# A chunked linear recurrence in a two-layer decoder trunk: the merge emitted ahead of the next preparation, and preparation and substitution emitted among the chunk loop

## The chip, the cores and the metric

The kernel runs on one core of a Trainium2 chip. The metric is the device time of one execution in microseconds (us). A core has five engines with queues of their own: TensorE (PE in the profile, its weight loads PEld), VectorE (DVE), ScalarE (ACT), GpSimd (POOL) and SyncE (SP). SP computes nothing here; it issues the DMA transfers. Each engine works off its own queue in the order in which the program put it there, and waits where an instruction needs a result or a buffer that is not there yet.

## The reference, cut to what matters

A trunk of two layers over 1024 positions of width 1024. Layer 0 mixes tokens by a gated MLP, layer 1 by a recurrence with a state of 64x64 per head (16 heads). Behind each mixer come a cross-attention and a SwiGLU feed-forward network. The change touches the recurrence of layer 1 alone:

```python
def rwkv7_recurrence(r, w, k, v, a, b):
    """S_t = S_{t-1} diag(w_t) + (S_{t-1} a_t) b_t^T + v_t k_t^T ;  y_t = S_t r_t."""
    def step(S, inp):
        r_t, w_t, k_t, v_t, a_t, b_t = inp
        sa = jnp.einsum('bhij,bhj->bhi', S, a_t)
        S = S * w_t[:, :, None, :] + sa[..., None] * b_t[:, :, None, :] + v_t[..., None] * k_t[:, :, None, :]
        return S, jnp.einsum('bhij,bhj->bhi', S, r_t)
    ...
    _, y = lax.scan(step, S0, xs)

def rwkv7_time_mix(...):
    ...
    y = rwkv7_recurrence(rh, decay, kh, vh, -kk, kk * ah)
    # group norm of y per head, bonus term, gate, output projection
    return (y * g) @ w_o, v_first
```

## The kernel before

The 1024 positions of the recurrence are cut into four batches b of 256 positions, and a batch into four chunks of 64. In a chunk the recurrence becomes matrix products once a triangular system of 64x64 per head and chunk is inverted. Heads are worked in pairs: eight pairs p, and groups pi of two pairs. Five steps, each a Python generator that stops (yields) after a small piece of work, make one batch:

- **Preparation** (`rwkv_prep`, L1280 to L1356), once per group pi: loads five inputs from DRAM (L1292), a running sum and exponentials (L1295, L1298), products (L1307 to L1311), then on PE the bonus sums (L1318), the score blocks (L1330, masked by DVE in L1333), transposes (L1337) and products with the values (L1354). The diagonal blocks of the triangular systems go to DRAM (L1343, L1344).
- **Substitution** (`rwkv_solve`, L1361 to L1385), once per batch: reads the diagonal blocks of all four groups back (L1366) and inverts the 32x32 triangles by 31 dependent steps of two DVE instructions each (L1376, L1377), then writes the result to DRAM (L1381, L1384).
- **Merge** (`rwkv_merge`, L1387 to L1423): reads the inverses back (L1393, L1398) and joins two 32x32 inverses to one of 64x64, by 64 and 64 products on PE (L1410, L1419; the profile counts each float32 product twice) with copies by ACT between them (L1413, L1422). The result lies in two buffers `Z` that all batches share.
- **Chunks** (`rwkv_chunks`, L1425 to L1482): 32 small chains per batch (four chunks by eight pairs), each a product with the state (L1446), an addition on DVE (L1447), a product with Z and further products (L1433), with ACT copying results and the new state (L1453, L1462, L1465). Chunk c of a pair needs the state that chunk c-1 left.
- **Post** (`rwkv_post`, L1484 to L1531): group norm of the outputs on DVE and POOL (L1498 to L1513), transposes on PE (L1520, L1527), the gate (L1528, L1529) and a store to DRAM.

Batch b's chunks need its merge, this its substitution, and this the whole preparation of the batch. The function `rwkv` (L1533) puts the steps in order. `run(g)` takes all pieces of a generator one after another and lets one piece of each waiting queue of tasks in behind each (`tick`); `later(g, q)` puts a generator into such a queue; `drain` empties the queues. What is emitted in this way is an order of priorities and no more: the framework's scheduler takes it together with its own model of times and of free buffers, and lays down each engine's queue from it. So instructions of one step can stand in a queue far ahead of steps that were emitted before it. Buffers that are reused (four PSUM banks `ps` for preparation and post, four `ck` for merge and chunks, 32 tiles `a`, seven `ld` and four `lx` for loaded inputs, one `invA` and one `invZ` that substitution and merge share) decide with it.

Of the kernel before, what the change touches and what calls it, by code (L numbers as in the profile page):

```python
# [21 lines left out]
class Trunk:  # L22
# [1510 lines left out]
    def rwkv(self, W, C, filler, mk_close):  # L1533
        nc = self.nc
        B = [self.rwkv_batch() for _ in range(4)]
        R, states = ({}, {})
        left, top, right = (ExitStack(), ExitStack(), ExitStack())

        def pools(stack, side, *nb):
            for n, bufs in nb:  # L1540
                R[n] = stack.enter_context(self.tc.tile_pool(name='r' + n, bufs=bufs, reuse_waits='tile', side=side))

        def stagger(gens, lag):

            gens = list(gens)
            done = [False] * len(gens)
            n = 0
            while not all(done):
                for i, g in enumerate(gens):
                    if n >= i * lag and (not done[i]):  # L1550
                        try:
                            next(g)
                        except StopIteration:
                            done[i] = True
                n += 1
                yield

        def prep(b):
            return stagger([self.rwkv_prep(R, B[b], pi, b, D_[0], C) for pi in range(4)], 7 if b else 6)

        def chunks(b):
            yield from self.rwkv_chunks(R, B[b], b, states)

        def post(b):
            return stagger([self.rwkv_post(R, B[b], pi, b, D_[0], C) for pi in range(4)], 2 if b == 3 else 1)

        def run(*gens, rate=1):
            for g in gens:
                for _ in g:
                    self.tick(rate)  # L1570

        def gated(half):

            xh, xl = self.chunks()
            for k in range(KD):
                t = R['ld'].tile([P, 512], F32, name='zt', tag='ld')
                nc.sync.dma_start(t, D_[0]['z'][k, :, half * 512:half * 512 + 512])
                self.split(xh[k], xl[k], t)
            return (xh, xl)
        D_ = []  # L1580

        def before_last():
            self.close_main()
            pools(left, 'left', ('inv', 1), ('D', 8))
            self.rwkv_consts(left.enter_context(self.tc.tile_pool(name='rconst', bufs=1, reuse_waits='tile', side='left')), C)
            pools(left, 'left', ('ld', 7))
            pools(top, 'left', ('tt', 4))
            self.open_main(2, 3, 2)
            self.open_psum(4, 4)
            self.later(prep(0))  # L1590
        d, gate_out = self.rwkv_project(W, C, filler, before_last, D_)
        self.drain()
        run(self.rwkv_solve(R, B[0]))
        p1 = prep(1)
        self.later(p1)
        gate_out()
        self.close_main()
        pools(top, 'left', ('bk', 4))
        pools(right, 'right', ('z', 1), ('st', 1), ('lx', 4))
        R['Z'] = [R['z'].tile([P, 2, 8, 64], F32, name=f'z{i}', tag=f'z{i}') for i in range(2)]  # L1600
        R['rs'] = [[R['st'].tile([P, P], F32, name='rs', tag=f'rs{h}{i}') for i in range(4)] for h in range(2)]
        for x in R['rs'][0] + R['rs'][1]:
            nc.gpsimd.memset(x, 0.0)
        for z in R['Z']:
            nc.gpsimd.memset(z[32:64, :, :, 0:32], 0.0)
            nc.gpsimd.memset(z[96:128, :, :, 0:32], 0.0)
        run(self.rwkv_merge(R, B[0]), p1)
        for b in range(1, 4):
            o = 3
            sv = self.rwkv_solve(R, B[b])  # L1610
            if o in (0, 1):
                run(sv, chunks(b - 1))
            elif o in (2, 3):
                run(chunks(b - 1), sv)
            else:
                self.later(sv)
                run(chunks(b - 1), rate=1)
                self.drain(0)
            self.later(post(b - 1), 1)
            if b == 3:  # L1620
                break
            if o in (0, 2, 4):
                run(self.rwkv_merge(R, B[b]))
            run(prep(b + 1), rate=1)
            if o in (1, 3, 5):
                run(self.rwkv_merge(R, B[b]))
            self.drain()
        top.close()
        self.open_main(2, 2, 1, 'left')
        gain, tmp = (self.gain_bc, self.tmp)  # L1630
        self.gain_bc = lambda row: gain(row, self.a32())
        self.tmp = self.a32
        for _ in range(2):
            self.tick()
        close = mk_close()
        x = gated(0)

        def between():
            run(self.rwkv_merge(R, B[3]))
            self.drain()  # L1640
            run(chunks(3))
            self.later(post(3), 1)
        first = self.out_half(x, 0, W['o'], close, 4, between)
        self.drain()
        self.open_psum(8)
        x = gated(1)
        self.later(first, 1)
        second = self.out_half(x, 1, W['o'], close)
        self.drain()
        self.gain_bc, self.tmp = (gain, tmp)  # L1650
        self.close_main()
        right.close()
        left.close()
        self.open_main(3, 4, 4, s7=2)
        self.later(second)
# [71 lines left out]
```

## Time and profile before

| | |
|---|---|
| median of three runs | 3225.27 us (3217.7 to 3227.76) |
| profiled execution, its own time | 3225.86 us |
| its span, first to last instruction | 3224.2 us |
| granted PE clock, mean | 0.966 |
| DVE, ACT, POOL busy | 1825.7, 1485.6, 824.9 us |

The loop over batches that the change rewrites lies between 1852 us and 2121 us of the span; the last merge and the last chunks (L1639 to L1641) follow, beside the output projection. In the profile a row of a list of groups has line, engine, operation, output and inputs, then the count, the busy time and the mean duration of one. A row of a list of instructions in order of time has start and duration, and in brackets how long the engine stood idle before it and what released it. In a table of stretches PEclk is the granted clock as a share of full speed.

### The profile page before, as it was taken

To read this page: it belongs to the slowest core of one execution; us is meant where nothing else is said; L and a number is where in the kernel's file an instruction comes from. 1 tells how busy PE (TensorE), PEld (TensorE's weight loads), DVE (VectorE), ACT (ScalarE), POOL (GpSimd) and SP (SyncE) were. 2 spreads that over 40 slices of the span, in tenths; PEclk is the share of its full clock that TensorE was granted. 3 is DMA by queue.
4 is the path that set the end of the run, shared out by engine and by line. 5 is a ranking of instruction groups with operands and counts; after the bars stand their busy time and mean duration, and the time that the engine had idled before them with its cause. 6 is when DMAs were issued, how large, how long until landed. Compare 5 with 4: busy or idle time off the path is not lost.

```text
span 3224.2 us, 43854 instructions
## 1 busy us (share of the span) xinstructions
PE 3085.9 (96%) x16570; PEld 2523.5 (78%) x16570; DVE 1825.7 (57%) x2562; ACT 1485.6 (46%) x2751; POOL 824.9 (26%) x646
## 2 busy tenths in 40 slices
PE   8999999899999999999989999999999899999998
PEld 6888888778888777878767778787788678888776
DVE  5563544565555476655765665664545755554656
ACT  5442544543333345666653445455545533333443
POOL 0100011355555100111421121223011555554001
PEclk9999999999999999999998888899999999999999
DMA  5622634423333644744857642535544333333633
GB/s 188 207 77 67 201 122 161 144 66 104 105 98 99 243 142 131 222 122 151 260 190 194 192 107 81 153 96 179 175 153 142 100 102 98 98 98 114 237 112 134
DMA packets 432499, 456.54 MB, mean 142 GB/s; under 512 B 77664, under 2 KB 307200, under 8 KB 432288
## 3 DMA queue, kind: packets, MB, share of 16 engines
q1 hardware_dynamic: 425376, 428.57, 42.2%
q0 software_dynamic: 6912, 25.17, 2.4%
q8 instruction: 131, 2.15, 0.3%
q14 instruction: 80, 0.66, 0.1%
HBM read 331.43 MB, written 122.22 MB: 141 GB/s over the span
## 4 chain that ended last, share of the span: by engine, by line
PE 83%; DVE 7%; DMA 4%; ACT 2%; issue 2%; POOL 1%; SPq 1%; DVEq 0%; POOLq 0%; ACTq 0%
PE ps L438 25%; PE ps L148 12%; PE ps L149 12%; PE ps L150 12%; PE ps L639 11%; PE ck L1433 4%; DVE wl L119 2%; PE ps L1330 2%; PE ck L1446 1%; PE ps L1354 1%; DVE a L119 1%; ACT wh L118 1%; PE ps L262 1%; DMA a<-scr 1%; PE ps L1337 1%
## 5 line engine op out<-in xcount | busy, mean ns | idle before, releaser
L438 PE MATMUL ps<-a,wh 128*128 128x512 f32 x2464 | 772.6, 399 | 7.2 <-DVE a L119 5.0
L119 DVE TENSOR_TENSOR wl<-wr,wh 128x1024 fp32r<-128x1024 f32 (+1 forms) x417 | 478.9, 1158 | 485.9 <-ACT wh L118 477.7
L118 ACT CAST wh<-wr 128x1024 fp32r<-128x1024 f32 (+1 forms) x417 | 371.3, 902 | 621.7 <-PE ps L639 172.6
L438 PEld LDWEIGHTS ps<-a,wh 128*128 128x128 f32 x2464 | 465.6, 189 | 125.6 <-DVE a L119 7.3
L438 PE MATMUL ps<-a,wl 128*128 128x512 f32 x1232 | 480.3, 398 | 0.0
L148 PE MATMUL ps<-a,wh 128*128 128x512 f32 (+1 forms) x848 | 329.1, 393 | 11.3 <-ACT a L118 8.0
L149 PE MATMUL ps<-a,wh 128*128 128x512 f32 (+1 forms) x848 | 326.2, 386 | 2.4 <-DVE a L119 2.4
L148 PE MATMUL ps<-wh,a 128*128 128x512 f32 x800 | 316.4, 403 | 12.3 <-DVE a L1528 3.9
L150 PE MATMUL ps<-a,wl 128*128 128x512 f32 (+1 forms) x848 | 325.0, 385 | 0.8 <-DVE wl L119 0.8
L149 PE MATMUL ps<-wl,a 128*128 128x512 f32 x800 | 319.2, 399 | 0.8 <-DVE wl L119 0.8
L150 PE MATMUL ps<-wh,a 128*128 128x512 f32 x800 | 317.2, 400 | 0.0
L208 POOL TENSOR_TENSOR sm<-sm,mhalf 128x4 f32<-128x4 f32 (+3 forms) x60 | 70.0, 1170 | 922.0 <-DVE sm L228 846.4
L438 PEld LDWEIGHTS ps<-a,wl 128*128 128x128 f32 x1232 | 233.2, 189 | 57.3 <-DVE wl L119 0.9
L639 PE MATMUL ps<-wl,wh 128*128 128x512 f32 x588 | 233.0, 396 | 11.6 <-DVE wl L119 11.6
L119 DVE TENSOR_TENSOR wl<-s,wh 128x512 fp32r<-128x512 f32 x176 | 201.1, 1156 | 68.4 <-ACT wh L118 64.7
L639 PE MATMUL ps<-wh,wl 128*128 128x512 f32 x588 | 230.9, 393 | 0.0
L639 PE MATMUL ps<-wh 128*128 128x512 f32 x588 | 195.3, 395 | 15.1 <-ACT wh L118 15.1
L118 ACT CAST wh<-s 128x512 fp32r<-128x512 f32 x176 | 106.3, 620 | 201.8 <-PE ps L438 66.9
L148 PEld LDWEIGHTS ps<-a,wh 128*128 128x128 f32 x848 | 163.0, 193 | 44.0 <-ACT a L118 9.0
L148 PEld LDWEIGHTS ps<-wh,a 128*128 128x128 f32 x800 | 152.3, 191 | 49.5 <-DVE a L1528 4.3
L150 PEld LDWEIGHTS ps<-a,wl 128*128 128x128 f32 x848 | 163.0, 192 | 35.4 <-DVE wl L119 2.3
L149 PEld LDWEIGHTS ps<-a,wh 128*128 128x128 f32 x848 | 163.4, 193 | 32.9 <-DVE a L119 2.7
(280 smaller groups left out, 5338.2 us busy)
## 6 DMA issues: line engine op xcount, KB each, us to landing
scr<-a SPq DMA_DIRECT2D x218, 256.0 KB
wr<-in_ffn_w_in SPq DMA_DIRECT2D x90, 512.0 KB
wr<-scr SPq DMA_DIRECT2D x70, 512.0 KB
scr<-t SPq DMA_DIRECT2D x60, 512.0 KB
wr<-in_rw_w_rkv SPq DMA_DIRECT2D x48, 512.0 KB
a<-in_ffn_w_out SPq DMA_DIRECT2D x40, 512.0 KB
t<-scr SPq DMA_DIRECT2D x36, 512.0 KB
ld<-scr SPq DMA_DIRECT2D x72, 256.0 KB
```

What stands on the lines that cost most here:

```text
L118: self.nc.scalar.copy(hi, src)
L119: (engine or self.nc.vector).tensor_sub(lo, src, hi)
L148: nc.tensor.matmul(out, lhsT=ah, rhs=bh, start=start, stop=False)
L149: nc.tensor.matmul(out, lhsT=ah, rhs=bl, start=False, stop=False)
L150: nc.tensor.matmul(out, lhsT=al, rhs=bh, start=False, stop=stop)
L208: self.nc.gpsimd.tensor_tensor(out=r, in0=v, in1=self.mhalf[:, 0:n], op=ALU.pow)
L262: nc.tensor.transpose(ps[:, t * P:(t + 1) * P], xs[t][:, k * P:(k + 1) * P], self.ident)
L438: self.nc.tensor.matmul(out, lhsT=a, rhs=b, start=start and k == 0 and (i == 0), stop=k == 3 and i == 2, skip_group_check=True)
L639: nc.tensor.matmul(ps, lhsT=a, rhs=b, start=i in (1, 2, 5) and n == 0 and k == 0 and z == 0, stop=n == NS - 1 and k == steps[n][1] - 1 and ...
L1330: nc.tensor.matmul(ps[:, c * P:(c + 1) * P], lhsT=BK[hs, q * 4 + c, :, :], rhs=AR[hs, q * 4 + c, :, :], start=True, stop=True)
L1337: nc.tensor.transpose(ps[:, c * P:(c + 1) * P], BK[:, q * 4 + c, :, :], self.ident)
L1433: mm = lambda o, l, r: nc.tensor.matmul(o, lhsT=l, rhs=r, start=False, stop=True, skip_group_check=True)
```

## The change

The loop over batches is written anew. Before, the order of emission for each b from 1 is: chunks of b-1, substitution of b, preparation of b+1 (with post of b-1 as a task beside it), merge of b. After, it is: post of b-1 becomes a task, merge of b, and then chunks of b with two pieces of "preparation of b+1, then substitution of b+1" behind each piece of chunks. The first batch's chunks and the second's substitution are emitted as before, and so are the third batch's post and what follows.

```diff
-        for b in range(1, 4):
-            o = 3
-            sv = self.rwkv_solve(R, B[b])
...
-            elif o in (2, 3):
-                run(chunks(b - 1), sv)
...
+        def beside(main, other):
+
+            for _ in main:
+                for _ in range(2):
+                    next(other, None)
+                yield
+            yield from other
+
+        def ahead(b):
+            yield from prep(b)
+            yield from self.rwkv_solve(R, B[b])
+        run(chunks(0), self.rwkv_solve(R, B[1]))
+        for b in range(1, 3):
             self.later(post(b - 1), 1)
-            if b == 3:
-                break
-            if o in (0, 2, 4):
-                run(self.rwkv_merge(R, B[b]))
-            run(prep(b + 1), rate=1)
-            if o in (1, 3, 5):
-                run(self.rwkv_merge(R, B[b]))
+            run(self.rwkv_merge(R, B[b]))
+            run(beside(chunks(b), ahead(b + 1)))
             self.drain()
+        self.later(post(2), 1)
```

No instruction that computes is added or removed: PE, DVE, ACT and POOL have as many as before. What changes is where they stand in the queues, at three places above all. In the rows below `x_...` is the tile that L1393 loads, `sm` small statistics, `a` a tile of the outputs, `invZ` and `invP` the tiles of the substitution, `ck` and `ps` PSUM banks.

PE's queue behind the chunks of batch 0, before:

```order
L1330 MATMUL ps<-ar,bk 128x128 x8
L1520 MATMUL ps<-ident,a 128x128 x4
L1527 MATMUL ps<-ident,a 128x128 x4
L1337 MATMUL ps<-ident,bk 128x128 x4
L1520 MATMUL ps<-ident,a 128x128 x4
L1410 MATMUL ck<-x_15494 32x32 x12
L1527 MATMUL ps<-ident,a 128x128 x4
L1330 MATMUL ps<-ar,bk 128x128 x4
```

And after:

```order
L1520 MATMUL ps<-ident,a 128x128 x4
L1527 MATMUL ps<-ident,a 128x128 x4
L1410 MATMUL ck<-x_14946 32x32 x64
L1520 MATMUL ps<-ident,a 128x128 x4
L1527 MATMUL ps<-ident,a 128x128 x4
L1419 MATMUL ck<-z_14040,x1t 32x32 x10
L1419 MATMUL ck<-z_14041,x1t 32x32 x2
```

The rows of preparation (L1330, L1337 and the rest of batch 2's 176 rows) that stood among post and merge are gone from here; the merge stands in one piece.

PE's queue within the chunks of batch 1, before:

```order
L1446 MATMUL ck<-s,ar 128x128
L1433 MATMUL ck<-rs,z_14040 64x64 x2
L1446 MATMUL ck<-s,ar 128x128 x2
L1433 MATMUL ck<-s,ident 128x128
L1433 MATMUL ck<-uv,gr 64x64 x2
L1433 MATMUL ck<-uv,bt 64x64 x2
```

And at the beginning of these chunks after:

```order
L1318 MATMUL ps<-sel,ld 128x2 x4
L1330 MATMUL ps<-ar,bk 128x128 x7
L1446 MATMUL ck<-s,ar 128x128 x3
L1330 MATMUL ps<-ar,bk 128x128
L1337 MATMUL ps<-ident,bk 128x128 x4
L1446 MATMUL ck<-s,ar 128x128
L1330 MATMUL ps<-ar,bk 128x128 x7
L1433 MATMUL ck<-rs,z_14040 64x64 x6
```

All 176 rows of batch 2's preparation now stand among the first 116 of the 256 rows of these chunks. In the next round the 176 rows of batch 3's preparation are split: 94 stand ahead of the merge of batch 2, 14 inside it, 13 between it and the first chunk, and 55 among the first 67 rows of the chunks of batch 2.

DVE's queue where the substitution of batch 2 ends, before (it is begun with the chunks of batch 1; eleven of its 62 rows are left behind the last L1447 of these):

```order
L1498 TENSOR_REDUCE sm<-ar 128x8
L1376 TENSOR_TENSOR invP<-invZ,invA 128x87
L1499 TENSOR_SCALAR sm<-sm 128x8
L1511 TENSOR_REDUCE sm<-ps 128x8
L1377 TENSOR_TENSOR invZ<-invZ,invP 128x29x3
L202 TENSOR_SCALAR sm<-sm 128x8
L1376 TENSOR_TENSOR invP<-invZ,invA 128x60
L1377 TENSOR_TENSOR invZ<-invZ,invP 128x30x2
```

And after, behind the last L1447 of the chunks of batch 1:

```order
L1376 TENSOR_TENSOR invP<-invZ,invA 128x220
L1528 TENSOR_TENSOR a<-a,ps 128x512
L1377 TENSOR_TENSOR invZ<-invZ,invP 128x22x10
L1309 TENSOR_TENSOR ar<-lx,tt 128x8x64
L1315 SCALAR_TENSOR_TENSOR ld<-ld,pcol,lx 128x256 x2
L1529 TENSOR_TENSOR a<-a,lx 128x512
L1376 TENSOR_TENSOR invP<-invZ,invA 128x207
L1528 TENSOR_TENSOR a<-a,ps 128x512
L1302 COPY D<-tt 128x8
L1377 TENSOR_TENSOR invZ<-invZ,invP 128x23x9
```

The substitution of batch 2 now begins behind 18 of the 32 L1447 of batch 1 (before: behind 6), 33 of its 62 rows stand behind the last of them, and among these 33 stand 43 rows of batch 1's post and batch 3's preparation. The first substitution (batch 1) stands nearly as it did.

More of the change, by code (lines that the diff above doesn't have):

```diff
@@ L1607, in rwkv @@
         run(self.rwkv_merge(R, B[0]), p1)
-        for b in range(1, 4):
-            o = 3
-            sv = self.rwkv_solve(R, B[b])
-            if o in (0, 1):
-                run(sv, chunks(b - 1))
-            elif o in (2, 3):
-                run(chunks(b - 1), sv)
[L1615 to L1618, printed above, removed]
-            self.later(post(b - 1), 1)
-            if b == 3:
-                break
-            if o in (0, 2, 4):
-                run(self.rwkv_merge(R, B[b]))
-            run(prep(b + 1), rate=1)
-            if o in (1, 3, 5):
-                run(self.rwkv_merge(R, B[b]))
+        def beside(main, other):
[9 more added lines that the diff above has]
+        for b in range(1, 3):
+            self.later(post(b - 1), 1)
+            run(self.rwkv_merge(R, B[b]))
+            run(beside(chunks(b), ahead(b + 1)))
             self.drain()
+        self.later(post(2), 1)
         top.close()
```

## The prediction, made before the changed kernel ran

> **What bounds the kernel now.** I read the page first (busy shares, then the chain that ended last), then a table of stretches over the loop, cut where PE's queue turns from one step to the next, and then the rows at those cuts.
>
> ```profile
> PE 3085.9 (96%) x16570; PEld 2523.5 (78%) x16570; DVE 1825.7 (57%) x2562; ACT 1485.6 (46%) x2751; POOL 824.9 (26%) x646
> PE 83%; DVE 7%; DMA 4%; ACT 2%; issue 2%; POOL 1%; SPq 1%; DVEq 0%; POOLq 0%; ACTq 0%
> ```
>
> PE is busy 96% and carries 83% of the chain, so an edit that keeps PE's work can win only where PE stands idle or runs at a lower clock. In the table below, from 1852.5 us, chunks of batch 0, then the way to batch 1's chunks (the first gap), chunks of 1, the second gap, chunks of 2, the output projection's first part, merge and chunks of 3:
>
> ```profile
> core 0: us, PE busy (x) PEld busy (x) DVE busy (x) ACT busy (x) POOL busy (x), PEclk, DMA share, GB/s
> 1852.50:1900.50 48.00, 46.59 (x515) 38.13 (x513) 31.86 (x98) 29.79 (x101) 3.93 (x4) 1.00 0.20 53
> 1900.50:1968.00 67.50, 62.32 (x586) 53.23 (x585) 39.08 (x89) 23.28 (x45) 23.07 (x19) 0.62 0.57 152
> 1968.00:2016.70 48.70, 47.57 (x537) 39.38 (x536) 32.78 (x99) 30.61 (x103) 3.81 (x4) 1.00 0.20 51
> 2016.70:2073.00 56.30, 51.36 (x581) 43.90 (x579) 33.07 (x80) 20.06 (x41) 20.81 (x18) 0.76 0.69 187
> 2073.00:2121.00 48.00, 46.81 (x506) 38.72 (x505) 34.13 (x98) 30.28 (x98) 2.25 (x2) 1.00 0.23 65
> 2121.00:2149.60 28.60, 27.91 (x169) 22.60 (x167) 22.47 (x39) 17.25 (x38) 16.03 (x10) 1.00 0.57 150
> ```
>
> The chunk stretches are full: at most 1.4 us of 48 idle, at full clock. That is against the change: the chunk loop looks like a latency chain in the code, but it has no holes for the preparation to fill. The waits of DVE say the same; its addition in the chain waits for PE:
>
> ```profile
> DVE rs L1447 <- PE ck L1446: 74.1, 44, 6.5
> ```
>
> The loss lies in the two gaps, 67.5 and 56.3 us, at a granted clock of 0.62 and 0.76. Each ends with the merge, which comes at the end of one chain: last step of the substitution on DVE, writes, reads, first product of the merge.
>
> ```profile
> 1904.71 0.21 DVE L1377 TENSOR_TENSOR invZ<-invZ,invP 128x31 f32<-128x31 f32 x1
> 1914.74 0.54 PE L1410 MATMUL ck<-x 32*32 32x32 f32 x24 [2.51 <-DMA x<-scr]
> 2021.12 0.21 DVE L1377 TENSOR_TENSOR invZ<-invZ,invP 128x31 f32<-128x31 f32 x1
> 2030.99 0.55 PE L1410 MATMUL ck<-x 32*32 32x32 f32 x24 [2.35 <-DMA x<-scr]
> ```
>
> From the end of the last step (1904.9, 2021.3) to the merge it takes 9.8 and 9.7 us, and PE then still has to work through the preparation that stands among the merge's products (up to 1968 and 2073).
>
> **The change, part by part.** No computing instruction is added, so every term is a shift. First the prices.
>
> ```profile
> L1330 PE MATMUL ps<-ar,bk 64*128 64x128 f32 x33 | 4.4, 287 | 0.0
> L1354 PE MATMUL ps<-uv,bk 128*64 128x64 f32 x34 | 2.8, 226 | 0.0
> L1419 PE MATMUL ck<-z,x1t 32*32 32x32 f32 x46 | 1.9, 196 | 0.0
> L1337 PE MATMUL ps<-ident,bk 128*128 128x128 f32 x8 | 1.3, 286 | 0.0
> L1318 PE MATMUL ps<-sel,ld 128*128 128x2 f32 x8 | 1.1, 254 | 0.0
> 2100.77 0.91 PE L1446 MATMUL ck<-s,ar 128*128 128x128 f32 x4
> 2115.13 0.92 PE L1446 MATMUL ck<-s,ar 128*128 128x128 f32 x4
> 2149.60 2.04 PE L1410 MATMUL ck<-x 32*32 32x32 f32 x62 [0.33 <-ACT a L1524]
> 2158.79 1.44 PE L1446 MATMUL ck<-s,ar 128*128 128x128 f32 x5
> ```
>
> The first five rows are PE's groups between 2057.7 and 2067.5, a dense stretch of 9.8 us: one group's preparation and 46 products of the merge. Without the merge's 1.3 (its share, less than the busy 1.9 since neighbours overlap) it is 8.5, so a batch's preparation is 4 x 8.5 = 34 us of PE (31.6 to 38.4, taking off all 1.9 or adding the busy sums). The two rows of L1446 are the first and last of six, 14.36 us for ten chains: 1.436 us each, 45.9 us for the 32 of a batch. The last two rows are the merge of batch 3, the one that stands in a piece before: 9.2 us from its first product to the first chunk.
>
> *First gap.* Batch 1's substitution keeps its place, so the merge still begins at 1914.7. It no longer carries preparation: 1914.7 + 9.2 = 1923.9 is where batch 1's chunks begin, 44 us earlier than 1968. But PE has nearly nothing to do from 1900.5 to 1914.7 except post. SP's queue changes here too: two of the merge's reads of Z now stand ahead of the read L1393 for which the merge waits, and the loads of post's values (L1495) that stood in between have gone further ahead.
>
> ```profile
> 1910.37 3.89 SPq L1398 DMA_DIRECT2D z<-scr  x6
> ```
>
> At 0.65 us an issue that is 1.3 us at most, and less the loads that left; I take 0. On POOL the clearing of the substitution's tile (L1368) now stands ahead of all but the first of the preparation's products L1311. It must wait for the merge, but the preparation on PE begins only then, so it costs nothing while that order holds.
>
> *Chunks of batch 1 with preparation of batch 2.* 45.9 + 34 = 79.9 us of PE, since neither has holes for the other. PE comes out of the gap at half clock:
>
> ```profile
> 1920.00:1930.00 10.00, 10.00 (x130) 8.13 (x130) 4.87 (x10) 3.62 (x8) 2.15 (x2) 0.55 0.71 177
> 1930.00:1940.00 10.00, 10.00 (x125) 8.71 (x122) 6.52 (x15) 4.74 (x10) 2.34 (x2) 1.00 0.65 205
> 1950.00:1960.00 10.00, 10.00 (x107) 8.83 (x106) 0.76 (x2) 4.21 (x8) 3.20 (x4) 0.50 0.38 99
> ```
>
> PE was dense from 1920 and had the full clock only about 9 us later; I charge 8 us at half speed, 4 us. The chunks end at 1923.9 + 79.9 + 4 = 2007.8 (before 2016.7): 8.9 us won.
>
> [...]
>
> *Second gap.* Here the substitution is late: batch 2's begins behind its preparation, in the midst of the chunks, and 33 of its 62 steps stand behind the last addition of the chunks, with 43 rows of post and preparation among them (before: 11 and 16 rows).
>
> ```profile
> L1376 DVE TENSOR_TENSOR invP<-invZ,invA 128x31 f32<-128x31 f32 (+15 forms) x31 | 10.8, 348 | 1.5 <-DMA invA<-scr 0.7
> L1377 DVE TENSOR_TENSOR invZ<-invZ,invP 128x31 f32<-128x31 f32 (+15 forms) x31 | 10.5, 337 | 0.7
> L1333 DVE TENSOR_TENSOR bk<-ps,mask 128x256 f32<-128x256 f32 x16 | 6.7, 418 | 16.4 <-PE ps L1330 16.4
> L1529 DVE TENSOR_TENSOR a<-a,lx 128x512 f32<-128x512 f32 x4 | 2.8, 689 | 0.1
> L1528 DVE TENSOR_TENSOR a<-a,ps 128x512 f32<-128x512 f32 x4 | 2.7, 687 | 3.9 <-PE ps L1527 2.4 <-issue 1.0 <-ACT a L1524 0.6
> L1315 DVE SCALAR_TENSOR_TENSOR ld<-ld,pcol,lx 128x256 f32<-128x256 f32 x6 | 2.6, 477 | 0.0
> L1309 DVE TENSOR_TENSOR ar<-lx,tt 128x512 f32<-128x512 f32 x3 | 2.1, 687 | 2.7 <-DMA lx<-scr 2.7
> L1295 DVE TENSOR_TENSOR_SCAN ld<-chunk_on,ld 128x512 f32<-128x512 bf16 x1 | 1.2, 1217 | 0.0
> L1499 DVE TENSOR_SCALAR sm<-sm 128x8 f32<-128x8 f32 x3 | 0.5, 165 | 0.0
> 2012.84 0.28 DVE L1447 TENSOR_TENSOR rs<-ck,uv 64x128 f32<-64x128 f32 x1
> ```
>
> The first two rows are the substitution of batch 1, the others from DVE's groups of the second gap. 33 steps x 0.343 = 11.3. The 43 rows: 8 of L1333 3.3, 8 of L1528 and L1529 5.5, 8 full-width ones of post (L1498, L1502, L1511) at the same 0.68 5.4, 4 of L1315 1.9, four more full-width products 2.9, L1295 1.2, ten small ones at 0.165 1.7: 22.0. Together 33.3 us if DVE waits for nothing. The last addition comes 3.6 us before the chunks' end (2013.1 against 2016.7), so at 2004.2; the substitution ends at 2037.5, 16 us later than before. PE's post and 94 rows of preparation (18 us) lie beside it and cost nothing, POOL's too. Then 9.7 to the merge (the same SP requests in a like order) and 9.2 to the chunks: 2056.4, against 2073.
>
> *Chunks of batch 2.* 68 of 176 rows of preparation still lie ahead: 13.1 us, before 2.1 (one block of L1354). So +11.0, and 4 again for the cold clock. Batch 3's substitution then begins in the midst of these chunks, and in DVE's queue only two additions stand between the last mask and its first step, which must wait for the blocks' way through DRAM:
>
> ```profile
> 1968.05 1.11 SPq L1343 DMA_DIRECT2D scr<-bk  x2
> 1975.27 0.17 DVE L1376 TENSOR_TENSOR invP<-invZ,invA 128x31 f32<-128x31 f32 x1
> ```
>
> 7.2 us, against 2 x 1.4 for the additions: PE's chunks behind it wait some 4 us, of which I take 3, since PE runs one chain ahead (bounds 0 and 4.4). Where batch 2's begins, three additions cover it; I take nothing.
>
> Sum at the end of batch 2's chunks: 2056.4 - 2073 = -16.6, +11.0 +4 +3 = +1.4 us. Behind that PE is full (27.91 of 28.6), so the shift goes through to the end. Batch 3's substitution ends about 10 us later than before; its merge began at 2149.6, and 9.7 behind 2123.9, the end of its last step, is 2133.6, so 16 us of slack cover it:
>
> ```profile
> 2123.73 0.22 DVE L1377 TENSOR_TENSOR invZ<-invZ,invP 128x31 f32<-128x31 f32 x1
> ```
>
> 3225.86 (the profiled execution, 0.6 above the median) + 1.4 = 3227.
>
> **The rivals.** *The waits don't come* (faster): DVE's rows overlap by some 0.08 us each (6 us over 76 rows), the clock recovers at once (8 less) and the first step finds its blocks (3 less): 17 less, 3210. For it: a chunk phase never left PE waiting before. Against it: 0.55 for 10 dense us. It decides if the granted clock in 1925 to 1935 is 1.00.
>
> *The substitution becomes the bound* (slower), one mechanism: it now stands in one DVE queue with post and preparation, so each of their waits is its own. The rows above give these: 3.9 (L1528), 2.7 (L1309), and of L1333's 16.4 a quarter (4 of 16 pairs stand there), 4.1: 10.7 more, 3238. It decides where DVE's idle time between the last L1447 and the last step exceeds 4 us. For it: before, only post's statistics stood there. Against it: POOL and PE now have less ahead of post.
>
> *The clock stays down* (slower): in 1950 to 1960 the same preparation ran dense at 0.50. The same rows took 67.5 us in one gap and 56.3 in the other; 11 us is the price in one round, 3238. Against it: the chunks, at 1.00 in all stretches, now stand among them.
>
> *The change does nothing*: the scheduler could lay the queues as before. The queues differ, so this has no chance of its own.
>
> **How the numbers follow.** About 0.3% (10 us) either side is what a measurement of this kernel can tell from no change. My forecast, a loss and a gain that cancel (3217 to 3235), 0.47. The first rival 0.24, the second 0.18, the third 0.11. So faster 0.24, same 0.47, slower 0.29. The range from 3209 to 3246 holds the forecast, the first rival's point and the second and third with half of the other's price on top; beyond lie both together, or more than all waits gone.
>
> **What the changed profile would show.** First L1410 of batch 1 still at 1914 to 1915 and first L1446 near 1924; chunks of 1 with preparation 80 to 84 us long with PE full; last L1377 of batch 2 near 2037 and DVE idle under 4 us in the 33 us before it; first chunk of batch 2 near 2056. I am wrong if chunks and preparation together take clearly less than 80 us, or if the substitution's tail is clearly off 33.

## The result, and the profile after

The changed kernel is slower (the forecast was 3227 us, in a range from 3209 to 3246): 3259.72 us in the median of four runs (3255.24 to 3265.99) against 3222.87 for the kernel before, a ratio of 1.012 (95% interval 1.0096 to 1.0144). The profiled execution took 3265.99 us, with a span of 3264.3 at a mean granted clock of 0.956 (before 3224.2 at 0.966). PE's busy time on the page grew with as many instructions:

```profile
PE 3113.3 (95%) x16570; PEld 2544.2 (78%) x16570; DVE 1826.8 (56%) x2562; ACT 1486.9 (46%) x2751; POOL 824.6 (25%) x646
```

27.4 us more of PE's busy time for the same 16570 rows: they ran slower. Stretches of the changed kernel, cut at the same events as those shown of before: chunks of batch 0, first gap, chunks of 1, second gap, chunks of 2, and the way to the last merge:

```profile
core 0: us, PE busy (x) PEld busy (x) DVE busy (x) ACT busy (x) POOL busy (x), PEclk, DMA share, GB/s
1849.00:1909.00 60.00, 57.23 (x569) 47.29 (x568) 38.74 (x114) 31.64 (x106) 7.91 (x6) 0.91 0.17 46
1909.00:1938.00 29.00, 21.14 (x338) 18.48 (x338) 15.96 (x31) 11.50 (x23) 12.04 (x11) 0.65 0.57 160
1938.00:2041.00 103.00, 100.02 (x773) 83.33 (x772) 46.35 (x127) 40.52 (x121) 12.91 (x11) 0.72 0.28 78
2041.00:2100.00 59.00, 46.35 (x518) 40.45 (x519) 42.45 (x100) 20.51 (x42) 19.97 (x17) 0.64 0.65 174
2100.00:2163.00 63.00, 61.77 (x613) 51.33 (x612) 37.09 (x103) 35.17 (x107) 2.17 (x2) 0.98 0.23 63
2163.00:2188.60 25.60, 23.32 (x131) 18.71 (x129) 21.06 (x42) 15.39 (x33) 14.99 (x10) 1.00 0.64 170
```

The third row is the one to look at. Chunks and preparation of batch 1 take 103 us with PE busy for 100, so nothing waits; but the granted clock is 0.72, and 100.02 x 0.28 = 28 us are lost. Cut finer:

```profile
1930.00:1940.00 10.00, 8.57 (x51) 7.36 (x49) 5.29 (x14) 1.29 (x4) 0.49 (x1) 0.67 0.41 135
1940.00:1950.00 10.00, 9.38 (x58) 7.32 (x57) 2.96 (x9) 3.80 (x12) 2.15 (x2) 0.50 0.45 121
1950.00:1960.00 10.00, 10.00 (x61) 8.80 (x59) 1.63 (x5) 2.16 (x6) 0.00 (x0) 0.50 0.09 28
1960.00:1970.00 10.00, 10.00 (x47) 7.97 (x48) 5.36 (x13) 2.63 (x8) 0.00 (x0) 0.50 0.34 105
1970.00:1980.00 10.00, 10.00 (x67) 8.41 (x65) 1.32 (x4) 3.40 (x9) 2.15 (x2) 0.50 0.21 46
1980.00:1990.00 10.00, 10.00 (x50) 8.51 (x52) 5.66 (x12) 2.53 (x7) 0.00 (x0) 0.50 0.31 88
1990.00:2000.00 10.00, 10.00 (x91) 9.04 (x89) 2.08 (x6) 3.45 (x9) 2.15 (x2) 0.67 0.34 91
2000.00:2010.00 10.00, 10.00 (x86) 8.28 (x83) 5.03 (x12) 4.18 (x13) 0.00 (x0) 1.00 0.28 82
```

For 40 us (1950 to 1990) PE is busy 10.00 of 10 at half clock, with 47 to 67 rows in ten microseconds where the chunks alone did 107. The forecast had charged 8 us at half speed. From 2000 to 2041 the rest of the mix, whose last rows of preparation stand at 2013, runs at 1.00 (39.23 of 41 us busy), so here it held that clock.

The whole execution can be split in this way: in stretches of 2 us, PE's idle time is length less busy time, the loss at low clock is busy time by one minus the granted clock, and what remains is work at full speed.

| kernel | ratio to before, 95% | profiled span | PE idle | loss at low clock | work at full speed |
|---|---|---|---|---|---|
| before | | 3224.2 | 138.3 | 92.1 | 2993.9 |
| after | 1.012 [1.0096, 1.0144] | 3264.3 | 151.0 | 122.0 | 2991.3 |
| e1 | 1.007 [1.0036, 1.0104] | 3242.6 | 143.1 | 96.7 | 3002.8 |
| e2 | 1.0079 [1.0054, 1.0105] | 3247.6 | 146.7 | 109.2 | 2991.7 |
| e4 | 1.0021 [0.999, 1.0051] | 3209.7 | 131.6 | 64.7 | 3013.4 |
| e5 | 1.0061 [1.004, 1.0082] | 3246.8 | 152.5 | 109.5 | 2984.8 |
| e6 | 1.0017 [0.9999, 1.0035] | 3224.3 | 149.2 | 83.3 | 2991.8 |
| e7 | 1.0079 [1.0051, 1.0107] | 3253.9 | 145.9 | 107.8 | 3000.2 |
| e8 | 1.0003 [0.9982, 1.0024] | 3238.1 | 149.7 | 97.0 | 2991.5 |
| e9 | 1.0165 [1.0128, 1.0201] | 3268.8 | 130.6 | 155.9 | 2982.3 |
| e10 | 1.0069 [1.0039, 1.0099] | 3251.3 | 150.6 | 106.5 | 2994.2 |
| e11 | 1.0 [0.9979, 1.0022] | 3219.2 | 152.4 | 77.9 | 2988.8 |
| e12 | 1.0047 [1.0025, 1.0069] | 3229.9 | 137.8 | 90.5 | 3001.6 |

The last column hardly moves where the products are the same (a spread of some 12 us is the error of the split). Before to after: 29.9 us at low clock, 12.7 us of idle PE. In the loop itself, from the first product of batch 0's merge to that of batch 3's, in stretches of 1 us:

| kernel | from, to | length | PE idle | loss at low clock | work at full speed |
|---|---|---|---|---|---|
| before | 1823.8, 2149.6 | 325.8 | 15.5 | 43.6 | 266.7 |
| after | 1824.1, 2188.6 | 364.5 | 31.3 | 70.6 | 262.6 |
| e6 | 1819.9, 2148.8 | 328.9 | 25.9 | 36.3 | 266.7 |
| e8 | 1815.7, 2137.8 | 322.1 | 26.4 | 25.0 | 270.8 |
| e9 | 1822.0, 2196.4 | 374.4 | 12.5 | 103.1 | 258.8 |

The two losses are what the experiments take apart. A span is that of one execution, the ratio that of all runs: e4's, e7's, e8's and e10's profiled executions lie some 10 to 20 us off their medians.

### The profile page after: what moved, and what is told of

The parts are those of the page before. It is cut to its first block, busy times and chain, and to the rows that moved or that the text cites. A ratio compares the mean times of both kernels' runs of the same rounds, so it can differ in the third digit from the quotient of the medians.

```text
span 3264.3 us, 43847 instructions
## 1 busy us (share of the span) xinstructions
PE 3113.3 (95%) x16570; PEld 2544.2 (78%) x16570; DVE 1826.8 (56%) x2562; ACT 1486.9 (46%) x2751; POOL 824.6 (25%) x646
## 4 chain that ended last, share of the span: by engine, by line
PE 40%; DVE 4%; DMA 2%; issue 1%; ACT 1%; POOL 1%; SPq 1%; DVEq 0%; POOLq 0%; ACTq 0%
PE ps L438 12%; PE ps L639 5%; PE ck L1433 4%; PE ps L150 4%; PE ps L148 4%; PE ps L149 4%; PE ps L1330 2%; PE ck L1446 1%; PE ps L1354 1%; DVE wl L119 1%; PE ps L1337 1%; DMA a<-scr 1%; PE ps L1318 1%; DVE a L119 1%; DMA ld<-scr 0%
```

## First experiments: the clock, or the late substitution?

**e1: 24 extra products in the merges of batches 1 and 2**, in the changed kernel, to fill the empty gap ahead of the mix.

```diff
+        if B.get('warm'):          # set for batches 1 and 2
+            ps = self.bank()
+            for _ in range(24):
+                nc.tensor.matmul(ps[:, 0:128], lhsT=self.ident, rhs=self.ident, start=True, stop=True)
```

> The changed kernel with 24 extra 128x128 products on TensorE (identity by identity, into a PSUM bank that nobody reads) in the merges of batches 1 and 2. In PE's queue 15 of the 24 stand ahead of the first merge and 9 behind its first half; all 24 ahead of the second. They fill time in which PE waits for the substitution, so their own cost is near 0 (bounds 0 and 24 x 0.29 = 7 us a round). Theory A, the mix of chunks and preparation cannot raise the granted clock from 0.50 by itself but keeps 1.00 once it has it: the first stretch of the mix, 101 us in the changed kernel, falls to 80 to 85 at a clock of 1.00, and the whole to 3225 to 3242. Theory B, the mix itself holds the clock at 0.50, however it begins: the stretch stays at 95 to 101 us and 0.50 shows again between 1940 and 1990, 3257 to 3270. Theory C, the loss lies in the late substitution and its waits, not in the clock: no gain either, 3257 to 3270, even where the clock shows 1.00.

Measured: 3244.29 us, a ratio of 1.007 in place of 1.012, 15 us less than the changed kernel: between the expectations. The stages say why. The first mix, the second gap, the second mix and the way to the last merge:

```profile
1929.90:2013.50 83.60, 81.07 (x817) 67.61 (x816) 52.62 (x136) 43.89 (x130) 13.56 (x13) 1.00 0.41 115
2013.50:2066.90 53.40, 46.08 (x548) 41.60 (x548) 39.30 (x94) 18.80 (x38) 19.23 (x16) 0.71 0.59 160
2066.90:2137.00 70.10, 69.27 (x607) 56.52 (x607) 34.38 (x97) 34.07 (x104) 2.98 (x3) 0.85 0.28 81
2137.00:2168.10 31.10, 25.82 (x157) 20.77 (x156) 29.08 (x56) 18.53 (x39) 13.96 (x10) 1.00 0.44 127
```

The first mix ran wholly at 1.00 and took 84 us instead of 103: theory A, mix as such does not force the half clock. But the second one fell back, out of dense work:

```profile
2060.00:2070.00 10.00, 10.00 (x200) 8.99 (x199) 6.46 (x18) 5.97 (x12) 2.88 (x4) 1.00 0.75 196
2070.00:2080.00 10.00, 10.00 (x107) 8.56 (x105) 1.89 (x6) 4.69 (x15) 0.00 (x0) 0.98 0.56 168
2080.00:2090.00 10.00, 10.00 (x56) 7.51 (x55) 0.76 (x2) 2.77 (x9) 0.00 (x0) 0.50 0.04 12
2090.00:2100.00 10.00, 10.00 (x68) 8.64 (x68) 2.33 (x7) 2.40 (x8) 0.00 (x0) 0.50 0.31 72
```

No gap stands ahead of the fall at 2079.7 us. So neither A (it keeps 1.00) nor B (it is held at 0.50) is the whole; and C is wrong, since time came back with the clock.

**e4: the same products in the kernel before** (the same edit).

> The kernel before with the same 24 extra products in the merges of batches 1 and 2. Here PE has less idle time in the gaps, and the queue has the products behind the merge (2 ahead of the end of the preparation, 22 behind, and all 24 behind it in the second), so they come too late to warm the stretch of preparation that ran at 0.50 to 0.63 between 1940 and 1960. Theory A: no gain, and 24 x 0.1 to 0.29 = 2 to 7 us of cost a round where no wait hides them: 3225 to 3237. Theory B and C: the same cost, the same range. What tells is only whether the clock of the chunk stretches behind them stays at 1.00.

Measured: 3230.71 us against 3220.31, not distinguishable from no change by the interval; its ten runs lie between 3211 and 3246. The profiled execution, its fastest, had the lowest loss at low clock of all (64.7 us). The products' own work (in the last column 19.5 us more here and 11.5 more in e1, with an error of some 12) takes away what they give.

**e2: the merge ahead of the preparation, and nothing interleaved by hand**, in the kernel before.

```diff
-            o = 3
+            o = 2
```

> One half of the change alone: the merge ahead of the next preparation, but the preparation whole behind it and ahead of the chunks, and the substitution behind the chunks' emission, with no interleaving by hand. The queue then has some 165 rows of preparation among the first 50 products of the chunks and the other 200 alone. Theory A and B (clock): PE comes out of the same empty gap at 0.50, so preparation (34 us at full clock) runs cold for a large part of its length and costs 15 to 25 us more in each round, against 9 us won by the earlier merge: 3240 to 3260. Theory C (the late substitution): the substitution of batch 2 begins right behind the preparation and is done within the chunks, so nothing is lost: 3215 to 3230.

Measured: 3249.38 us, in the range of the clock theories and far from C's. From the merge to 1945, the first mix, the second gap, the second mix:

```profile
1923.10:1945.00 21.90, 21.90 (x330) 19.97 (x331) 11.14 (x27) 8.75 (x16) 4.48 (x6) 0.50 0.67 193
1945.00:2020.00 75.00, 74.19 (x745) 61.94 (x744) 44.76 (x119) 38.60 (x116) 10.13 (x9) 0.99 0.35 94
2020.00:2064.40 44.40, 32.60 (x417) 28.19 (x417) 29.08 (x67) 17.29 (x35) 17.08 (x14) 0.63 0.51 145
2064.40:2139.00 74.60, 73.72 (x716) 62.46 (x716) 46.09 (x128) 38.11 (x116) 5.45 (x5) 0.93 0.36 103
```

The gap of 44 us has 12 us of idle PE (4.9 before). That half of the change alone costs most of the loss: 0.8 of the 1.2%.

**e5: four steps of preparation and substitution to one piece of the chunks**, in the changed kernel.

```diff
-                for _ in range(2):
+                for _ in range(4):
```

> The changed kernel with four steps of preparation and substitution to one piece of the chunks in place of two, so that the substitution ends sooner. Theory C: the second gap shrinks by the part of the substitution's tail that now lies beside the chunks, 15 to 25 us: 3235 to 3245. Theory A and B: the same empty gap ahead of the mix and the same rows in it, with the clock at 0.50 for the first 40 to 60 us of each round; only the second gap is shorter, so 3240 to 3258, with 0.50 in the ten-microsecond stretches of the first mix.

Measured: 3240.73 us, within both ranges. The split speaks for the clock: idle time did not fall (152.5 us), the loss at low clock did (109.5). The profile shows 0.50 twice (in stretches of 2 us from 1926 to 1950 and from 1976 to 1992), the second time behind 1.1 us of idle PE:

```profile
1926.10:1955.00 28.90, 28.90 (x392) 25.86 (x392) 10.92 (x27) 11.23 (x23) 5.33 (x6) 0.56 0.58 162
1955.00:1974.00 19.00, 17.85 (x190) 15.34 (x188) 14.25 (x33) 8.46 (x22) 4.39 (x4) 1.00 0.48 137
1974.00:1992.00 18.00, 18.00 (x101) 15.46 (x101) 6.07 (x16) 5.23 (x14) 0.00 (x0) 0.54 0.44 111
```

## Second experiments: what holds the clock down

In e1 products of 128x2 (L1318) and the score blocks L1330, which use 64 rows of PE's array (`64*128` in the prediction's table of groups, L1446 `128*128`), stood ahead of the fall, beside the first products of the chunks (L1446). So the next edit leaves the count and the columns of the products alone and changes the rows that they use. It changes one thing more: the scheduler laid PE's queue anew for e6, e8 and e9, as the order of PE's rows in their traces shows. What holds where the order is the same stands behind e8.

**e6: L1330 over 128 partitions**, in the changed kernel.

```diff
-  nc.tensor.matmul(ps[:, c * P:(c + 1) * P], lhsT=BK[hs, q * 4 + c, :, :], rhs=AR[hs, q * 4 + c, :, :], ...)
+  nc.tensor.matmul(ps[:, c * P:(c + 1) * P], lhsT=BK[:, q * 4 + c, :, :], rhs=AR[:, q * 4 + c, :, :], ...)
```

> The changed kernel with the preparation's products L1330 taken over all 128 partitions, two heads at once, in place of the 64 of one head: as many instructions, as many columns, the same waits, only twice the rows of the array in use (the values of its output are then not the reference's). In the run with the extra products the granted clock fell to 0.50 at 2079.7 us although PE had been busy without a gap for 20 us; the 3.5 us ahead of the fall held products of 128x2 (L1318) and of 64 rows (L1330), and the next rise came behind L1354's. Theory D, the clock follows how much of the array the products use, so light products keep it down: the first mix recovers much sooner, its stretch of 101 us falls to 80 to 90, the whole to 3230 to 3245. Theory E, only the idle gap ahead of the mix and the moment in which a busy stretch begins count, not the rows: no change, 3253 to 3267.

Measured: 3225.38 us in ten runs (3219.98 to 3236.76), none of them near the changed kernel's 3255 to 3266: 34 us less, 5 us below theory D's range. First mix, second gap, second mix:

```profile
1922.00:2002.00 80.00, 78.33 (x806) 67.18 (x804) 48.87 (x129) 40.65 (x121) 12.57 (x11) 0.99 0.37 103
2002.00:2067.50 65.50, 53.60 (x601) 49.20 (x603) 45.28 (x110) 24.25 (x49) 19.34 (x15) 0.74 0.59 162
2067.50:2123.00 55.50, 54.35 (x524) 44.80 (x519) 36.43 (x105) 31.55 (x99) 3.21 (x4) 0.88 0.27 82
```

And the group of these products in a stretch at full clock, 1940 to 1960 us (count, busy time, mean ns):

```profile
L1330 PE MATMUL ps<-ar,bk 128*128 128x128 f32 x48 | 6.8, 285 | 0.0
```

285 ns over 128 rows, 287 over 64 in the kernel before: the edit makes no product faster. It takes 38.7 us off the loss at low clock and 1.8 off the idle time.

**e10: half the dose**, 128 rows for one head of two.

```diff
+                    rw = hs if h else slice(0, 128)
-  ... lhsT=BK[hs, q * 4 + c, :, :], rhs=AR[hs, q * 4 + c, :, :], ...
+  ... lhsT=BK[rw, q * 4 + c, :, :], rhs=AR[rw, q * 4 + c, :, :], ...
```

> Half the dose in the changed kernel: L1330 over 128 partitions for one head of two, over 64 for the other (the values of its output are then not the reference's). All of them over 128 took 34 us off. Theory D with a measure that adds up: about half, 3238 to 3247. Theory D with a threshold that the mix lies just below: nearly all of it, 3225 to 3237. Theory E: none, 3253 to 3267.

Measured: 3242.5 us, 17 of the 34. That looks like an effect that adds up, but the trace doesn't show one. PE's queue here is the changed kernel's until the first mix, and within the mix 54 of its 762 rows stand elsewhere. In this first mix half the dose did nearly what the whole did in e6: from the first L1446 to the last it took 79 us instead of 105 (75 in e6). Half of that was lost again in the second gap, from there to the next L1446 (75 us instead of 63). The first mix and the start of the second gap:

```profile
1938.00:2018.00 80.00, 77.58 (x784) 64.94 (x784) 47.24 (x123) 40.94 (x122) 14.53 (x12) 0.99 0.35 96
2018.00:2050.00 32.00, 25.21 (x119) 21.71 (x119) 26.14 (x55) 9.73 (x21) 14.79 (x11) 0.50 0.44 132
```

From the second gap on e10's queue differs from the changed kernel's. It is e6's from within the first mix on, over 1326 rows of PE, which took 141 us in e6 and 150 in e10. So the whole dose did about as much as the half at first and more behind it; whether the clock follows a threshold or a sum stays open. That more rows in L1330 alone bring this mix from 0.72 to 0.99 is shown here with nearly the same order of PE's rows, in one execution of each.

**e9: the opposite edit in the kernel before**: L1354 over the 64 rows that hold values.

```diff
-  nc.tensor.matmul(ps[0:64, o:o + 64], lhsT=GA[:, h, q * 4 + c, :], rhs=UV[:, q * 4 + c, h, :], ...)
+  nc.tensor.matmul(ps[0:64, o:o + 64], lhsT=GA[64:128, h, q * 4 + c, :], rhs=UV[64:128, q * 4 + c, h, :], ...)
```

> The opposite edit, in the kernel before: the preparation's last products L1354 taken over the 64 rows that hold values (the other 64 hold zeros, so the result stays the same); as many instructions and columns. Theory D, the clock follows how much of the array the products use: the stretches of preparation become lighter, the clock recovers later, and the kernel before gets slower, 3235 to 3255, with its loss at low clock (PE's busy time by one minus the granted clock, 92 us in the profiled execution before) at 105 to 120. Theory E: no change, 3216 to 3230.

Measured: 3271.33 us, 54 more than the kernel before and beyond even theory D's range; slower than the changed kernel. The loss at low clock went from 92.1 to 155.9 us; idle time fell. The preparations, and the chunks behind each:

```profile
1940.00:1990.00 50.00, 50.00 (x305) 44.16 (x302) 20.50 (x50) 13.98 (x27) 6.09 (x7) 0.51 0.46 128
1990.00:2040.00 50.00, 49.10 (x498) 40.64 (x499) 33.28 (x103) 28.97 (x100) 1.96 (x2) 0.87 0.14 40
2070.00:2120.00 50.00, 50.00 (x304) 44.61 (x303) 14.27 (x36) 10.42 (x21) 4.08 (x5) 0.50 0.42 120
2120.00:2170.00 50.00, 49.29 (x483) 40.48 (x483) 36.89 (x105) 30.17 (x99) 3.20 (x4) 0.91 0.22 67
```

The program emits its steps as in the kernel before, and PE is dense; but the scheduler laid the queue otherwise from the 353rd row behind the first L1318 on. In the 352 rows of PE ahead, whose order is the same, the mean granted clock is 0.79 here and 0.85 in the kernel before. As the rows left out multiply zeros, the result is unchanged, so the values of the result have no part in it. Theory E, that only gaps and moments count, is contradicted from both sides; how much of the 54 us is the rows and how much the new order stays open. (The edit also takes away L1354's wait for POOL's clearing of the zero half; that by itself can only shorten waits.)

**e8: L1330 over 128 partitions in the kernel before** (the edit of e6).

> The kernel before with the same edit: L1330 over 128 partitions (the values of its output are then not the reference's). Theory D: the stretches of preparation at 0.50 to 0.63 (1940 to 1960, and the start of the second gap) come at a higher clock, 5 to 15 us less: 3205 to 3216. Theory E: no change, 3218 to 3230.

Measured: 3220.15 us against 3222.72, no change: a miss for theory D in the time, though not in the clock. In the loop the loss at low clock fell from 43.6 to 25.0 us, as D has it, but PE's idle time rose from 15.5 to 26.4. PE now waits more in the gaps; its longest waits between 1900 and 2070 us (total, times, longest), of which the first is new and the other two were 4.1 and 4.9 us before:

```profile
PE ps L1354 <- DMA uv<-scr: 5.4, 2, 4.5
PE ps L1337 <- DVE sm L1511: 4.4, 2, 2.4
PE ck L1410 <- DMA x<-scr: 4.2, 2, 2.5
```

Net, the loop became 3.7 us shorter. Then, in the profiled execution, the last batch's chunks ran at half clock, though no L1330 stands among them; first that stretch, then the same one of the kernel before:

```profile
2149.00:2205.00 56.00, 56.00 (x336) 45.00 (x337) 6.79 (x24) 18.93 (x64) 1.04 (x1) 0.50 0.03 11
```

```profile
2159.00:2202.00 43.00, 43.00 (x438) 35.98 (x439) 8.91 (x34) 23.54 (x82) 3.07 (x3) 0.94 0.14 43
```

So the chunks' products, too, stayed at 0.50, dense, for 56 us. All of them use 128 rows (`128*128` and `128*64` in the profile's groups), so the rows in use are not the whole of what the clock followed here; what else counts is open. The ten runs of e8 lie 27 us apart.

**Rows or order?** From the first L1318 on, 1056 rows of PE (the preparation of batch 0, the first merge and most of the preparation of batch 1 among them) come in the same order in e6 as in the changed kernel, and in e8 as in the kernel before. This stretch in before, after, e6 and e8:

```profile
1707.00:1844.70 137.70, 130.76 (x1056) 110.86 (x1056) 84.38 (x186) 53.03 (x95) 22.86 (x37) 0.86 0.74 200
1707.80:1844.40 136.60, 131.13 (x1055) 110.66 (x1055) 84.08 (x186) 51.15 (x92) 23.58 (x37) 0.86 0.74 201
1707.20:1837.50 130.30, 120.99 (x1055) 106.17 (x1056) 84.68 (x186) 50.96 (x92) 22.93 (x37) 0.93 0.75 208
1704.00:1839.10 135.10, 123.60 (x1056) 108.87 (x1056) 85.01 (x186) 52.69 (x95) 22.66 (x37) 0.91 0.75 202
```

With L1330 over 64 rows the mean granted clock is 0.86, over 128 rows 0.93 and 0.91. The other profiles agree: 0.84 to 0.87 over as many rows in the six that have L1330 over 64 rows and L1354 over 128, 0.94 in e10, 0.92 in e11. So the direction of the effect is shown at the same order. Of the whole 34 us of e6, the share of the rows and that of the new order were not separated.

**e7: e1 and e5 together; e11: e6 and e5 together; e12: 16 products on the last state behind the chunks**, in the kernel before, to fill the gaps from their beginning.

```diff
+            if b < 3:                                                        # e12
+                ps = self.bank()
+                for _ in range(16):
+                    nc.tensor.matmul(ps[:, 0:128], lhsT=self.ident, rhs=states[7], start=True, stop=True)
             self.later(post(b - 1), 1)
```

> Both repairs together: four steps of preparation to one piece of the chunks, and the 24 extra products in the merges of batches 1 and 2. Apart they gave 3241 and 3244. If clock and late substitution are two separate losses, the gains add: of the 39 us, 19 and 15 come back, 3222 to 3232. If the four-to-one order already gained by its clock (its loss at low clock was 123 us against 134), the gains overlap: 3232 to 3242.

> The changed kernel with L1330 over 128 partitions (the values of its output are then not the reference's) and four steps of preparation to one piece of the chunks. If the 19 us that four to one won by itself came from an earlier substitution, they come on top of the 34: 3205 to 3213. If they came from the clock, which the 128 rows have put right already, nothing is added: 3218 to 3232.

> The kernel before with 16 extra products of 128x128 on TensorE right behind the last chunk of batches 0 and 1 (they read the last state, so that they cannot move ahead, and nobody reads them). PE stands idle for 5 us of the 20 behind the chunks. If they keep the clock up through the gap, the 25 us of PE's work that run at low clock in the two gaps shrink by 8 to 15 against 2 to 4 us of added work: 3209 to 3219. If the light products behind bring the clock down in any case: the cost alone, 3223 to 3232.

Measured: e7 3244.7 us, no better than either part and worse than both expectations (the losses that its expectation gives as 123 and 134 us are 109.5 and 122.0 by the split above); e11 3220.51, so that with the clock put right four to one adds at most a few us (5 to e6, within the spread of its runs); e12 3234.18, 17 more than before, just above its costs. Warming products do not pay here: e12's loss at low clock is 90.5 us against 92.1. They come too early: in both gaps PE still stood idle for 4.84 us behind them, waiting for DVE's part of post, and in this time the clock fell (at 1905.6 and 2025.1 us). So e12 doesn't test whether light products bring it down.

```profile
1907.13 1.11 PE L1337 MATMUL ps<-ident,bk 128*128 128x128 f32 x4 [4.84 <-DVE sm L1511]
2025.86 1.11 PE L1337 MATMUL ps<-ident,bk 128*128 128x128 f32 x4 [4.84 <-DVE sm L1511]
```

No version beats the kernel before.

## Why the prediction was wrong, point by point

- **The step that failed** is "I charge 8 us at half speed, 4 us". In 1938 to 2041 the low clock cost 28 us. With that the mix took 108 us from its first L1446 (1931.5) to the end of its last addition (2039.5), against 80 in the forecast (1923.9 to 2004.2). The rival "the clock stays down" had the right mechanism (0.67 in 1920 to 1940, then 0.50), at 11 us and a chance of 0.11; what spoke against it, "the chunks, at 1.00 in all stretches, now stand among them", was the false reason: the changed kernel at 1850 us and e8 show the chunks themselves at 0.50. The price came from the difference of two gaps that both ran cold; the other bound, all of the mix's 79.9 us at half clock, would have been 79.9 us more and was not put into the range.
- **The other two rivals** did not come, by the signs that they had named: the clock in 1925 to 1935 was 0.66 and not 1.00, and DVE stood idle for 1.7 us of the substitution's tail, not for more than 4.
- **Where the time went**: the first chunk of batch 2 came at 2099.4 instead of 2056.4. Of these 43.0 us, 5.8 lie ahead of the first merge, 1.7 between it and the first chunk, 27.8 in the mix, 0.4 in the tail, 2.6 on the way to the second merge and 4.7 from there to the chunks.
- **The 8 us of recovery** came from one stretch of the kernel before (0.55 in 1920 to 1930), when a row of 10.00 busy us at 0.50 (1950 to 1960) stood in the same fence. So PE had been dense and slow in the forecast's own numbers, and the consequence was not drawn.
- **Chunks and preparation have no holes for each other**: right. 100.02 x 0.72 = 72 us of full-speed work in that stretch (76 from the first L1446 on), and 81.07 at 1.00 in e1, against 79.9.
- **The substitution's tail, 33.3 us**: right in kind, and the number partly by luck. Last addition of the chunks, last step, merge:

```profile
2039.22 0.28 DVE L1447 TENSOR_TENSOR rs<-ck,uv 64x128 f32<-64x128 f32 x1
...
2073.03 0.21 DVE L1377 TENSOR_TENSOR invZ<-invZ,invP 128x31 f32<-128x31 f32 x1
2085.51 1.72 PE L1410 MATMUL ck<-x 32*32 32x32 f32 x112
```

  The step ends 33.7 us behind the addition's end (2073.2 against 2039.5). The forecast added up the rows' times and left out overlap and waits. In the trace the 76 rows add up to 36.9 us, since four of them took 1.0 to 1.5 us each; they overlap by 4.9, and DVE was idle for 1.7. To the merge 12.3 us (forecast 9.7), and from there 14 to the first chunk (forecast 9.2), at a clock of 0.74 and with 13 rows of preparation that the forecast had charged to the chunks. So the second gap took 59 us against 48.6 forecast, 12.7 of them idle (4.9 before), as no preparation is left to fill it.
- **The first merge at 1914.7**: it came at 1920.5. The chunks of batch 0 already ran 10 us at half clock (in e1, e2, e5 and e7 too, which share the changed kernel's queue there; 1.00 in the kernel before, in e4 and in e12). The code ahead is the same, a few rows of the queue differ; whether they are the cause was not tried.

```profile
1850.00:1860.00 10.00, 10.00 (x55) 8.66 (x54) 3.88 (x10) 2.24 (x5) 0.00 (x0) 0.50 0.30 74
```

- **The chunks of batch 2**: 63.0 us, forecast 66 (48 + 11 + 4 + 3). The wait of the first step, taken as 3, didn't come: in the whole stretch PE stands idle for 1.2 us (61.77 of 63 busy), as before (46.81 of 48). Nor did the second 4 us for a cold clock: at 0.98 it cost 1.2.
- **Lateness goes through to the end**: right. 39.0 us at the last merge (2188.6 against 2149.6), 40.1 at the end of the span.

## What to carry to other kernels

A busy PE isn't a PE at speed (here 100 of 103 us busy at 0.72): read the granted clock beside the busy share in every stretch, and price an edit that mixes stages by what clock each product mix held before, at both levels. Here the products L1330 took as much time over 64 rows of the array as over 128 (287 and 285 ns), but with the same order of rows the mean clock over 1056 rows was 0.86 with the one and 0.93 and 0.91 with the other. When work is moved out of a gap, price the stage behind the gap too: here PE was left busy for 21.14 of 29 us at 0.65, and in the next stage the low clock cost 28 us. And when an edit is to change one thing alone, compare the queues first: a scheduler can lay them anew for a change in one operand.

## What the runs showed of the hardware that was not expected

- Less loss at low clock came with more waits: e8's loop had 18.6 us less of the one and 10.9 us more of the other, so a stretch's loss at low clock is no promise of as much gain.
- A dense PE stayed at 0.50 for 40 us and more in the changed kernel, for 50 us in e9 and 56 us in e8 (busy 56.00 of 56), and fell from 1.00 to 0.50 without any gap in e1 (at 2079.7 us).
- Twice the rows in L1330: 34 us off; in half of them: 17 off; half the rows in L1354: 54 us on, each with what the scheduler made of the queue. With the same order of rows the mean clock was 0.93 and 0.91 instead of 0.86 over 1056 rows. Durations at full clock stayed as they were (285 and 287 ns for L1330). Whether the small blocks of the merge (32x32), the transposes L1337 and the products of 128x2 act in the same way was not tried.
- The kernel before, run 67 times beside the experiments on two chips, lies between 3204 and 3247 us, and the mean granted clock goes with it: 3204 us at 0.974, 3247 at 0.958. In the profiles of the changed kernel and of e5, 1950 rows from the first L1318 on come in the same order, and the mean clock over them is 0.85 and 0.81. So the clock differed between executions of one kernel, and over one order of rows, and a few runs say less than they seem to.
